# Hybrid attention and mLSTM encoder on one core: PSUM banks of the neighbourhood attention dealt out anew

## The chip, the cores and the metric

The kernel runs on one core of a Trainium2 chip. The metric is the device time of one execution in microseconds (us); "before" is the median of three runs. The core has a matrix engine (TensorE, PE in the profile), three engines for elementwise work (VectorE = DVE, ScalarE = ACT, GpSimd = POOL) and SyncE (SP), which issues most DMA transfers. PE writes its results to PSUM, which is used here as eight banks of 512 fp32 values for each of 128 partitions. DVE and ACT read them from there.

## What is computed

One encoder layer over two sequences, of 1024 and 2048 tokens, with 16 learned tokens put ahead of each. One projection feeds two branches, a 2-D neighbourhood attention and a bidirectional mLSTM; both are gated, projected, merged and sent through an output projection. The change is in the attention, which in the reference is:

```python
def row_block(r):
    r0 = jnp.clip(r - wr // 2, 0, rows - wr)
    k_blk = lax.dynamic_slice_in_dim(kg, r0, wr, axis=1)[:, :, kc]
    v_blk = lax.dynamic_slice_in_dim(vg, r0, wr, axis=1)[:, :, kc]
    s_win = jnp.einsum('bcqhd,bwckhd->bhcqwk', q_blk, k_blk).astype(jnp.float32) * scale
    s_win = jnp.where(valid[:, :, None, :], s_win + bias, NEG)
    s_met = jnp.einsum('bcqhd,bmhd->bhcqm', q_blk, km).astype(jnp.float32) * scale
    p = jax.nn.softmax(jnp.concatenate([s_met, s_win], axis=-1), axis=-1).astype(v.dtype)
    ...
    return (jnp.einsum('bhcqm,bmhd->bcqhd', p_met, vm)
            + jnp.einsum('bhcqwk,bwckhd->bcqhd', p_win, v_blk))
```

The tokens form a grid 64 wide. Each has 8 heads of 64 and looks at a window of 8 rows by 16 columns and at the 16 learned tokens.

## The kernel before

Two generators make the program. One is "dense": the projections, the gates, the merge and the output (`PLAN`), all with accumulations in three banks, pj. The other is "sparse": the mLSTM and the attention of the short sequence, then those of the long one (`STEPS`). `run` takes a piece of the sparse work, which gives its cost in us, and then dense pieces worth that much, so that attention and dense matmuls lie between each other on PE. PE executes them in just the order of the code. The orders of ACT, DVE, POOL and SP come from a scheduler, which works with estimated times when the program is built (`tc.manual_schedule(engines={PE})`, `schedule_with_timeline_sim=True`). So these orders can differ from the code's. The eight PSUM banks are named by tag:

```python
BANKS = dict(pj=3, tr=2, sc=1, sm=2)
```

`psum(tag, shape)` takes a bank of a tag; where a tag has two banks, the scheduler gives the one that comes free first by its estimate, and makes the first write wait for the last reader of what lay there.

The attention (`na`, with `STEPS`: two row tiles of the short sequence, four of the long one) works in units. A row tile is 8 grid rows; a unit is one tile, one head and one block of 16 columns: 128 queries. Each head of each tile has four units, so there are 64 units for the short sequence and 128 for the long one. A round of the loop over u has four steps, each followed by dense work of some us:

1. In odd rounds the sums of the finished pair are copied (`na_copy`, L1295, ACT). `na_scores` of unit u: it takes a bank and makes two matmuls (L1241, L1242) of split-precision queries and keys; DVE adds the bias in place and finds the extreme value (L1245). At the first unit of a head, `na_prep` starts the loads and splits of the next head (stk, kx, vr: L1189 to L1226).
2. `na_exp` of unit u on ACT reads the bank and writes prb to SBUF (L1256). This is the last read of the scores' bank. `na_scale` of unit u-1 on DVE (L1265, L1266). In odd rounds the two adds of the finished pair (`na_add`, L1302, DVE), the last reads of the sums' bank.
3. `na_turn` of unit u-2: three or four transposes on PE of prb into a bank (L1273), and an ACT copy of it to pts (L1275).
4. `na_low` of unit u-2 on DVE, the rest of the split (L1280), the last read of the transposes' bank. `na_out` of unit u-3: three or four matmuls (L1288), which sum values over the weights pts. Two units share one bank; it is taken in odd rounds.

The two calls that take banks for scores and transposes, and the one for the sums:

```python
self.turns = not self.turns
sc = self.psum("sc" if self.turns else "sm", [P, 512])      # na_scores
pt = self.psum("tr", [P, 4, P])                             # na_turn
pairs[u - 3] = self.psum("sm", [P, 512])                    # na, odd rounds
```

So even units' scores lie in sc, odd units' in one of the two sm, from which the sums also take theirs. The mLSTM (`ml`, between the attentions and ahead of the first) uses sc, tr and sm too. Its transfers are issued by `self.mq`, which is GpSimd for the long sequence and SyncE for the short one, in both kernels.

Of the kernel before, what the change touches and what calls it, by code (L numbers as in the profile page):

```python
# [3 lines left out]

# [1 line left out]

# [12 lines left out]
P = 128  # L19
# [56 lines left out]
def _row_types(R):  # L76

    out = []
    for t in range(R // 8):
        if t == 0:  # L80
            out.append((0, 0, 11))
        elif t == R // 8 - 1:
            out.append((2, R - 12, 12))
        else:
            out.append((1, 8 * t - 4, 15))
    return out
# [52 lines left out]
class K:  # L139
# [3 lines left out]
    def __init__(self, tc, ins, outs):  # L143
        self.tc, self.nc = tc, tc.nc
        self.xs = []
        self.i, self.o = ins, outs
        self.wreq, self.wraw, self.wrdy, self.wout = deque(), deque(), deque(), 0
        self.wseen, self.wkept, self.xkept = set(), {}, {}
        self.rwait = {}
        self.xput, self.turn, self.last, self.turns = deque(), 0, None, False  # L150
        self.marks, self.loose = {}, True
        self.need = False
        self.hold, self.early = deque(), True
        self.sides, self.qd, self.TD = [], {}, {}
# [949 lines left out]
    def na(self, s, rts):  # L1104

        tc, nc, i = self.tc, self.nc, self.i
        rows = _row_types(SEQLEN[s] // 64)
        with tc.tile_pool(name=f"na{s}{rts[0]}", bufs=1, side="right", reuse_waits="tile") as np_:
            self.qB = [np_.tile([P, 4, P], F32R, name=f"qB{j}") for j in range(2)]
            self.kx = [np_.tile([P, 16, 64], F32R, name=f"kx{j}") for j in range(2)]  # L1110
            self.gts = [np_.tile([P, 17, 48], F32, name=f"gt{j}") for j in range(2)]
            for q in self.qB:
                nc.gpsimd.dma_start(q[64:128], i["onehot"].rearrange("a (b c) -> a b c", b=4))
            for g in self.gts:
                nc.gpsimd.memset(g[:, 0, :], 0.0)
                nc.gpsimd.memset(g[:, 16, :], 0.0)
            heads = [(rt, pr, hh) for rt in rts for pr in range(4) for hh in range(2)]
            n = len(heads)
            prep = self.na_prep(np_, s, rows, heads, 0)
            self.na_bias(rows, heads, 0)  # L1120
            for k in range(6):
                next(prep, None)
                for _ in range(2 if k else 17 - 5 * s):
                    yield A_N[s]
            cur, nxt = self.head, None
            units = [(j, cb) for j in range(n) for cb in range(4)]
            ready = {}
            n_ = len(units)
            pairs = {}
            for u in range(n_ + 4):  # L1130
                if u >= 5 and u % 2:
                    self.na_copy(ready[u - 5], pairs[u - 5])
                    if u > n_:
                        self.na_add(ready[u - 5], pairs.pop(u - 5), s)
                if u < n_:
                    j, cb = units[u]
                    if cb == 0:
                        cur = self.head
                        prep = self.na_prep(np_, s, rows, heads, j + 1) if j + 1 < n else iter(())
                        next(prep, None)  # L1140
                    ready[u] = [cur, heads[j], cb, None, None, self.gts[j % 2], None]
                    self.na_scores(np_, ready[u], rows)
                    if j + 1 < n and cb == 0:
                        self.na_bias(rows, heads, j + 1)
                yield A_N[s]
                if u < n_:
                    self.na_exp(np_, ready[u])
                if 1 <= u <= n_:
                    self.na_scale(np_, ready[u - 1])
                if 5 <= u <= n_ and u % 2:  # L1150
                    self.na_add(ready[u - 5], pairs.pop(u - 5), s)
                if u < n_ and cb:
                    next(prep, None)
                if u == n_ + 3:
                    break
                yield A_N[s]
                if 2 <= u <= n_ + 1:
                    self.na_turn(np_, ready[u - 2])
                    if u < n_ and cb >= 2:
                        next(prep, None)  # L1160
                yield A_N[s]
                if 2 <= u <= n_ + 1:
                    self.na_low(ready[u - 2])
                if u >= 3:
                    if u % 2:
                        pairs[u - 3] = self.psum("sm", [P, 512])
                    self.na_out(ready[u - 3], pairs[(u - 3) // 2 * 2])
                yield A_N[s]
# [61 lines left out]
    def na_scores(self, np_, unit, rows):  # L1230
        nc = self.nc
        (stk, qb, kd, vt, yg, zt), (rt, pr, hh), cb = unit[:3]
        gt, c0 = unit[5], OFFC[cb] + 1
        typ, _, nr = rows[rt]
        ns = nr + 1
        kc, nb, g0 = KC0[cb], NKB[cb], (5, 1, 0)[typ]
        w, N = 8 * nb, 8 * nb * ns
        self.turns = not self.turns
        sc = self.psum("sc" if self.turns else "sm", [P, 512])
        so = sc[:, :N].rearrange("p (a b) -> p a b", b=w)  # L1240
        nc.tensor.matmul(so, stk[:, cb, :], kd[:, :ns, kc:kc + w], start=True, stop=False)  # L1241
        nc.tensor.matmul(so, qb[:, cb, :], self.kx[hh][:, :ns, kc:kc + w], start=False, stop=True)  # L1242
        pr_ = np_.tile([P, 512], F32, name="prb", bufs=3)
        mx = np_.tile([P, 1], F32, name="mx", bufs=4)
        nc.vector.tensor_tensor_reduce(  # L1245
            out=so, in0=so, in1=gt[:, g0:g0 + ns, c0:c0 + w],
            op0=ALU.add, op1=ALU.min, scale=-1.0, scalar=3.0e38, accum_out=mx)
        unit[3] = (pr_, mx, nb, 8 * ns)
        unit[6] = sc
# [18 lines left out]
    def na_turn(self, np_, unit):  # L1268
        nc = self.nc
        pr_, _, nb, ks = unit[3]  # L1270
        pt = self.psum("tr", [P, 4, P])
        for ch in range(nb):
            nc.tensor.transpose(pt[:ks, ch, :], pr_[:, ch * ks:(ch + 1) * ks], self.ident)  # L1273
        pts = np_.tile([P, 4, 2, P], F32R, name="pts", bufs=2)
        nc.scalar.activation(pts[:ks, :nb, 0, :], pt[:ks, :nb], AF.Copy)  # L1275
        unit[4], unit[6] = pts, pt
# [931 lines left out]
```

## Time and profile before

| | |
|---|---|
| median of three runs | 2667.29 us (2664.7 to 2668.91) |
| the profiled execution's own time | 2669.63 us |
| its span, first to last instruction | 2667.9 us |
| PE / DVE / ACT / POOL busy | 2633.8 / 1912.9 / 1422.4 / 365.8 us |
| mean granted clock of PE | 0.998 |
| DMA | 800.48 MB, mean 300 GB/s |
| attention of the short sequence: first to last scores | 822.0 to 1160.5 us |
| attention of the long sequence: first to last scores | 1918.4 to 2543.4 us |

The profile is of one execution. Times of rows are us from the span's start; where a row of a group gives a mean, it is in ns. In a row of the timeline stand start, length, engine, line, operation, what is written and read, and how many instructions are merged; in brackets, the idle time before it and what ended that. Matmuls overlap and their ends are modelled, so an idle time of PE is somewhat smaller than the time lost. A row of the windows view gives, for a stretch, its length and the busy time of PE, PE's weight loads, DVE, ACT and POOL with their instructions in parentheses, then PE's granted clock, the busy share of the DMA engines and GB/s.

### The profile page before, as it was taken

The numbers are of one execution on the slowest core, as the hardware profiler recorded it, in microseconds if no ns is written. First come the engines' busy times: TensorE is split into PE (matmuls) and PEld (weight loads), VectorE is DVE, ScalarE is ACT, GpSimd is POOL, SyncE is SP. The second block draws the span as 40 slices with busy tenths as digits, with TensorE's granted clock in tenths as the row PEclk, the third lists the DMA queues.
The fourth block names the chain that finished last, engine by engine and source line by source line (L and its number), as shares of the span: only waits on it lengthen the run. The fifth ranks groups of instructions, "written<-read, shape, count | busy, mean of one in ns | idle before, by whom it ended". The sixth has DMA issues, their size and how long they took to land.

```text
span 2667.9 us, 46714 instructions
## 1 busy us (share of the span) xinstructions
PE 2633.8 (99%) x15928; PEld 2326.9 (87%) x15928; DVE 1912.9 (72%) x5082; ACT 1422.4 (53%) x3292; POOL 365.8 (14%) x670
## 2 busy tenths in 40 slices
PE   9999999999999999999999999999999999999998
PEld 7998897889988999888888888888889898989888
DVE  5655678778776877546676776767478979797854
ACT  5423555544445555546665666656456555656521
POOL 0111130001301124002222222222000000000000
PEclk9999999999999999999999999999999999999999
DMA  9899988799866999978889998899899898998965
GB/s 374 329 332 338 331 298 305 276 327 351 313 215 240 353 323 307 319 226 278 260 276 363 347 287 257 283 351 355 281 308 326 276 288 277 282 310 268 333 238 203
DMA packets 346990, 800.48 MB, mean 300 GB/s; under 512 B 50016, under 2 KB 119664, under 8 KB 342912
## 3 DMA queue, kind: packets, MB, share of 16 engines
q1 hardware_dynamic: 301632, 659.35, 73.2%
q0 software_dynamic: 45120, 138.15, 15.2%
q8 instruction: 126, 2.06, 0.3%
q14 instruction: 112, 0.92, 0.1%
HBM read 543.72 MB, written 253.60 MB: 299 GB/s over the span
## 4 chain that ended last, share of the span: by engine, by line
PE 91%; DMA 4%; DVE 3%; ACT 2%; issue 1%; SPq 0%; DVEq 0%; ACTq 0%
PE pj L218 11%; PE pj L220 10%; PE pj L219 10%; PE pj L988 7%; PE pj L990 7%; PE pj L989 7%; PE pj L787 5%; PE pj L789 5%; PE pj L788 5%; PE pj L1955 3%; PE sm L1288 3%; PE pj L1954 3%; PE pj L1956 3%; PE tr L1273 2%; DMA whl<-w 1%; DMA stk<-nq 1%
## 5 line engine op out<-in xcount | busy, mean ns | idle before, releaser
L218 PE MATMUL pj<-xh,whl 128*128 128x512 f32 (+1 forms) x960 | 368.6, 384 | 2.7 <-DMA whl<-w 1.4
L220 PE MATMUL pj<-xh,whl 128*128 128x512 f32 (+1 forms) x960 | 360.4, 375 | 0.0
L219 PE MATMUL pj<-xl,whl 128*128 128x512 f32 (+1 forms) x960 | 359.8, 375 | 0.2 <-DVE xl L446 0.2
L787 PE MATMUL pj<-whl,xh 128*128 128x256 f32 (+1 forms) x1152 | 329.1, 286 | 1.7 <-DMA whl<-w 1.7
L789 PE MATMUL pj<-whl,xl 128*128 128x256 f32 (+1 forms) x1152 | 325.3, 282 | 0.0
L788 PE MATMUL pj<-whl,xh 128*128 128x256 f32 (+1 forms) x1152 | 324.9, 282 | 0.0
L1954 PE MATMUL pj<-whl,mh 128*128 128x256 f32 x768 | 218.9, 285 | 1.1 <-DMA whl<-w 1.1
L787 PEld LDWEIGHTS pj<-whl,xh 128*128 128x128 f32 x1152 | 217.1, 188 | 2.3 <-DMA whl<-w 1.9
L788 PEld LDWEIGHTS pj<-whl,xh 128*128 128x128 f32 x1152 | 217.0, 188 | 0.2
L789 PEld LDWEIGHTS pj<-whl,xl 128*128 128x128 f32 x1152 | 217.0, 188 | 0.0
L1955 PE MATMUL pj<-whl,mh 128*128 128x256 f32 x768 | 216.9, 282 | 0.0
L1956 PE MATMUL pj<-whl,mlo 128*128 128x256 f32 x768 | 216.0, 281 | 0.0
L220 PEld LDWEIGHTS pj<-xh,whl 128*128 128x128 f32 x960 | 180.9, 188 | 34.9
L218 PEld LDWEIGHTS pj<-xh,whl 128*128 128x128 f32 x960 | 180.8, 188 | 34.3 <-ACT xh L445 2.2
L988 PE MATMUL pj<-xh,whl 128*128 128x512 f32 x512 | 207.0, 404 | 1.6 <-ACT pj L1005 1.3
L219 PEld LDWEIGHTS pj<-xl,whl 128*128 128x128 f32 x960 | 181.3, 189 | 30.4 <-issue 1.0
L990 PE MATMUL pj<-xh,whl 128*128 128x512 f32 x512 | 202.0, 394 | 0.0
L989 PE MATMUL pj<-xl,whl 128*128 128x512 f32 x512 | 201.1, 393 | 0.0
L1275 ACT ACTIVATE pts<-tr 96x384 fp32r<-96x384 f32 (+2 forms) x192 | 103.4, 538 | 117.4 <-PE tr L1273 116.7
L1280 DVE TENSOR_TENSOR pts<-tr,pts 96x384 fp32r<-96x384 f32 (+2 forms) x192 | 118.6, 618 | 59.9 <-ACT pts L1275 58.3
L218 PE MATMUL pj<-yh,whl 128*128 128x512 f32 x384 | 154.1, 401 | 0.0
L219 PE MATMUL pj<-yl,whl 128*128 128x512 f32 x384 | 151.5, 394 | 0.7 <-DVE yl L1856 0.7
(387 smaller groups left out, 6993.1 us busy)
## 6 DMA issues: line engine op xcount, KB each, us to landing
whl<-w SPq DMA_DIRECT2D x131, 1024.0 KB
whl<-q SPq DMA_DIRECT2D x112, 512.0 KB
w<-whl SPq DMA_DIRECT2D x36, 1024.0 KB
wraw<-wu SPq DMA_DIRECT2D x48, 512.0 KB
gt<-st SPq DMA_DIRECT2D x96, 256.0 KB
tg<-gt SPq DMA_DIRECT2D x96, 256.0 KB
q<-po POOLq DMA_DIRECT2D x26, 512.0 KB, 7.1
xt<-xt SPq DMA_DIRECT2D x24, 512.0 KB
```

The source lines that it names most:

```text
L218: mm(out, ah, bh, start=start, stop=False)
L219: mm(out, ah, bl, start=False, stop=False)
L220: mm(out, al, bh, start=False, stop=stop)
L787: nc.tensor.matmul(o, xh, wh, start=k == 0, stop=False)
L788: nc.tensor.matmul(o, xh, wl, start=False, stop=False)
L789: nc.tensor.matmul(o, xl, wh, start=False, stop=k == KT - 1)
L988: mm(bank, w[:, 0, k], xh[:, k], start=fresh and k == 0, stop=False, skip_group_check=True)
L989: mm(bank, w[:, 0, k], xl[:, k], start=False, stop=False, skip_group_check=True)
L990: mm(bank, w[:, 1, k], xh[:, k], start=False, stop=k == 3, skip_group_check=True)
L1954: nc.tensor.matmul(o, mh[:, k, xs], wh, start=clear > 0 and k == 0, stop=False)
L1955: nc.tensor.matmul(o, mh[:, k, xs], wl, start=False, stop=False)
L1956: nc.tensor.matmul(o, ml[:, k, xs], wh, start=False, stop=clear < 2 and k == KT - 1)
```

## The change

Scores and transposes take one bank each in turn from sc, tr, tr; the turn begins anew with each call of `na`. Only the sums of pairs still take sm in the attention. The transposes' tile is now a 512 wide bank seen as 4 x 128. The number of banks for each tag, the mLSTM and the dense work stay as they are, and so does the long mLSTM's `self.mq`.

```diff
-from itertools import chain
+from itertools import chain, cycle
...
-        self.xput, self.turn, self.last, self.turns = deque(), 0, None, False
+        self.xput, self.turn, self.last = deque(), 0, None
...
                 nc.gpsimd.memset(g[:, 16, :], 0.0)
+            self.banks = cycle(("sc", "tr", "tr"))
             heads = [(rt, pr, hh) for rt in rts for pr in range(4) for hh in range(2)]
...
         w, N = 8 * nb, 8 * nb * ns
-        self.turns = not self.turns
-        sc = self.psum("sc" if self.turns else "sm", [P, 512])
+        sc = self.psum(next(self.banks), [P, 512])
         so = sc[:, :N].rearrange("p (a b) -> p a b", b=w)
...
         pr_, _, nb, ks = unit[3]
-        pt = self.psum("tr", [P, 4, P])
+        pt = self.psum(next(self.banks), [P, 512]).rearrange("p (a b) -> p a b", a=4)
         for ch in range(nb):
             nc.tensor.transpose(pt[:ks, ch, :], pr_[:, ch * ks:(ch + 1) * ks], self.ident)
```

In the prediction S(u) stands for the scores of unit u, T(u) for its transposes; "sums" are the matmuls of L1288.

## The prediction

> **What bounds the kernel now.** I read the page's head first, then the stages, then what TensorE (PE) waited for.
>
> ```profile
> PE 2633.8 (99%) x15928; PEld 2326.9 (87%) x15928; DVE 1912.9 (72%) x5082; ACT 1422.4 (53%) x3292; POOL 365.8 (14%) x670
> ```
>
> Of the 2667.9 us span PE is busy for all but 34 us. No other engine can gain the kernel more than PE's waits and its slow-clock time hold. The two attention stages:
>
> ```profile
> 820.00:1135.00 315.00, 314.72 (x2152) 291.45 (x2151) 230.05 (x522) 172.13 (x340) 63.78 (x112) 1.00 0.91 314
> ...
> 1905.00:2565.00 660.00, 651.78 (x4229) 589.33 (x4228) 533.86 (x1258) 382.06 (x871) 2.06 (x4) 1.00 0.93 291
> ```
>
> In the short one (820 to 1135) PE idles 0.3 us, in the long one (1905 to 2565) 8.2 us. The view of PE's waits (us in total, times, longest) says on whom, for 1900 to 2560:
>
> ```profile
> PE sm L1288 <- ACT prb L1256: 3.8, 6, 1.2
> PE sm L1288 <- DVE yg L1302: 3.6, 3, 2.5
> PE sm L1288 <- DVE pts L1280: 0.9, 1, 0.9
> ```
>
> They are all of the stage's waits, ten, and all are of L1288, the attention's sums. Six end with an exponential on ScalarE (ACT; prb, L1256), three with an add of finished sums on VectorE (DVE; yg, L1302), one with the sums' own data (pts, L1280). Only the last is a need for data. The other nine wait for a bank: L1256 is the last reader of a score bank, L1302 of a sum bank, so the sums do take banks which scores have just left.
>
> ```profile
> L1241 PE MATMUL sc<-kd,stk 128*128 128x288 f32 (+2 forms) x96 | 32.8, 342 | 0.0
> ...
> L1241 PE MATMUL sm<-kd,stk 128*128 128x384 f32 (+2 forms) x96 | 32.6, 340 | 0.0
> ```
>
> Of 192 units' scores, 96 lie on sc and 96 on sm, where the sums also go. The transposes, on tr, stand in no row of the waits.
>
> **What one such wait costs.** The longest, and the clock around it:
>
> ```profile
> 2170.24 0.60 PE L1273 MATMUL tr<-ident,prb 128*128 128x128 f32 x4
> 2173.32 0.59 PE L1288 MATMUL sm<-pts,vt 128*128 128x256 f32 x3 [2.48 <-DVE yg L1302]
> ...
> 2177.51 0.28 PE L1955 MATMUL pj<-whl,mh 128*128 128x256 f32 x1
> 2177.63 0.28 PE L1956 MATMUL pj<-whl,mlo 128*128 128x256 f32 x1
> ...
> 2178.45 0.60 PE L1273 MATMUL tr<-ident,prb 128*128 128x128 f32 x4
> 2178.80 0.36 PE L1954 MATMUL pj<-whl,mh 128*128 128x256 f32 x1
> ```
>
> ```profile
> 2172.75 0.42 DVE L1302 TENSOR_TENSOR yg<-sm,yg 64x256 f32<-64x256 f32 x1
> ```
>
> ```profile
> 2170.00:2175.00 5.00, 2.52 (x18) 2.32 (x17) 4.46 (x10) 3.30 (x7) 0.00 (x0) 0.89 1.02 369
> 2175.00:2180.00 5.00, 5.00 (x35) 5.00 (x35) 2.54 (x8) 2.02 (x7) 0.00 (x0) 0.77 1.02 232
> ```
>
> The add ends at 2172.75 + 0.42 = 2173.17, the sum starts at 2173.32. After four transposes the next matmul normally starts 0.35 later (2178.45 to 2178.80), so here at 2170.59: the loss is 2.73, 0.25 more than the 2.48 shown, since matmul ends are modelled. After a projection matmul (0.28 long, next one 0.12 later) a wait hides 0.16. So the nine hide 1.4 to 2.3; three follow transposes and six a projection matmul, which gives 1.7. Then the clock sinks: the granted share, 0.89 and 0.77 in two stretches of 5 us, gives 5 x 0.11 + 5 x 0.23 = 1.7 us of lost clock. So this wait cost 4.4 us in all.
>
> [...]
>
> **The change part by part.**
>
> 1. PE's stream is the code's own order and no matmul, copy or DMA is added, removed or moved, on SP's and POOL's queues neither; the loads of the long mLSTM are not in the diff. What can change are waits, and through them the order that the scheduler gives ACT and DVE.
>
> 2. Sums get both sm banks alone. A pair of units holds one for two units' time, so the next pair takes the other, last read two pairs before. How long before that one was read out, at the tightest of the long stage's 62 pairs:
>
> ```profile
> 2110.87 0.41 DVE L1302 TENSOR_TENSOR yg<-sm,yg 64x256 f32<-64x256 f32 x1
> ...
> 2119.56 0.72 PE L1288 MATMUL sm<-pts,vt 128*128 128x256 f32 x4
> ```
>
> 2119.56 - 2111.28 = 8.3 us. All nine waits go: 3.8 + 3.6 = 7.4 shown and 1.7 hidden are 9.1 us. With the 2.48 goes its slow spell, 1.7. Gross: **10.8 us**. What is late next at these places is the sums' data, as at 2166.61 below.
>
> 3. Scores and transposes share three banks in the order S(u), T(u-2), S(u+1), T(u-1), S(u+2). Every bank is taken again at the third take. S(u+2) gets the bank of T(u-2), whose last reader is the subtraction L1280; the sum of unit u-2 stands ahead of S(u+2) on PE and needs that subtraction anyway, so this wait is free. T(u-1) gets the bank of S(u) and waits for its exponential: this is new. Behind a waiting transpose PE holds the projections, everything else in its queue. Before, the bank of an even unit's scores was next needed by S(u+2), two steps later; an odd unit's by the sums of its own round, three steps earlier. So odd units gain time, even units lose some. How much is left, with the rows as they stand:
>
> ```profile
> 2146.70 0.67 ACT L1256 ACTIVATE prb<-sc,mx 128x512 f32<-128x512 f32 x1
> 2148.68 0.60 PE L1273 MATMUL tr<-ident,prb 128*128 128x128 f32 x4
> ...
> 2177.73 0.58 ACT L1256 ACTIVATE prb<-sc,mx 128x384 f32<-128x384 f32 x1 [3.81 <-DVE mx L1245]
> 2184.07 0.49 PE L1273 MATMUL tr<-ident,prb 128*128 128x128 f32 x3
> ```
>
> Over the long stage's 126 units, from the end of exponential u to the start of T(u-1), the tightest is the first pair, 2148.68 - 2147.37 = 1.3 us, the widest the second, 2184.07 - 2178.31 = 5.8; ten lie under 3. None is negative, so as they stand the new waits cost 0. Bounds: 0 below (a wait cannot gain), above the 16 us of the slow rival. The row to go by is the kernel's one wait for pts, 0.9 + 0.16: I take one such wait more, **1.1 us**, for the new order on ACT and DVE.
>
> 4. Something is bound to the DMAs rather than to PE:
>
> ```profile
> 2110.00:2160.00 50.00, 49.15 (x291) 42.56 (x290) 45.10 (x100) 24.35 (x52) 0.00 (x0) 1.00 1.02 319
> ...
> 2163.57 0.63 ACT L1208 ACTIVATE qB<-stk 64x512 fp32r<-64x512 f32 x1 [4.88 <-DMA stk<-nq]
> ...
> 2166.61 0.62 PE L1288 MATMUL sm<-pts,vt 128*128 128x256 f32 x3 [0.92 <-DVE pts L1280]
> ```
>
> ACT stood 4.88 us for stk, in the stretch where the DMA engines were full (share 1.02). PE's 2166.61 wait follows from it. A gain made inside that stretch meets the same landing and comes back as a longer wait there. From 2110 to 2160 PE's waits are this one:
>
> ```profile
> PE sm L1288 <- ACT prb L1256: 0.8, 1, 0.8
> ```
>
> With its hidden 0.16, **1.0 us** is given back. The earlier gains lie before 2110; I take it that their shift reaches the DMAs too.
>
> 5. The long mLSTM between the attention stages keeps its banks' names, but its ACT and DVE order may shift. Its neighbour of the same kind bounds it:
>
> ```profile
> PE sm L220 <- DVE ktl L1579: 4.9, 3, 2.6
> ```
>
> ```profile
> PE sm L220 <- DVE ktl L1579: 0.7, 2, 0.4
> ```
>
> 0.7 us now, 4.9 in the short mLSTM: from -0.7 to +4.2. I take 0, its own row.
>
> Sum: 10.8 - 1.1 - 1.0 = 8.7 us less. From the profiled execution's own 2669.63: 2660.9. That execution lies 2.3 above the median of the three runs, 2667.29, and its slow spell (1.7) may be part of the difference. From the median, 8.7 less gives 2658.6; if the median's run never had the spell, 2660.3 and, at the most, 2660.9. I forecast **2659.8**, 0.28% under the median.
>
> **The rivals.**
>
> *Given back (faster by less than 0.2%, 2663.4).* The waits are symptoms of late ACT and DVE, and PE meets them again at pts. For it:
>
> ```profile
> 2210.00:2260.00 50.00, 48.80 (x256) 40.81 (x256) 47.36 (x112) 27.30 (x58) 0.00 (x0) 1.00 0.87 284
> ```
>
> ```profile
> PE sm L1288 <- ACT prb L1256: 1.2, 2, 0.7
> ```
>
> DVE was busy 47.4 of 50 us here (waits in the second row), 45.1 in the stretch of 2110 to 2160. If it is the bound there, the waits in both stretches stay (0.8 + 1.2 + 3 x 0.16 = 2.5), and the 4.4 of 2173.32, whose root is the stk landing, returns as wait for pts: 6.9 of the 10.8 stay, 3.9 are gained, 2663.4. Against it: over the stage DVE is busy 533.9 of 660, and at 2173.32 pts had long been made.
>
> *The transposes pay (slower).* If the exponentials end later against PE by a fixed lag, the shortfalls of the 126 units add to 7.3 us for a lag of 3.0, 15.2 for 3.6 and 20.5 for 3.8. It decides from 3.6 on: 16 us eat the 10.8 and 0.2%. At 3.8: 2667.3 - 10.8 + 20.5 = 2677.0. For it: without the bank waits PE no longer pauses for ACT. Against: a lag of 3.6 is as much as the widest 5.8 down to 2.2, in all units at once, and ACT is idle 278 of 660 us.
>
> *The clock trips more often (2674).* If transposes stop PE for short whiles in each turn of the three banks, PE may sit at half clock again and again. A wait of 2.5 with its spell costs 4.4; four in place of the nine give 17.6 - 10.8 = 6.8 more. Against: waits up to 1.2 were followed by no slow spell here, and five banks left the clock at 1.00 over the long stage, rounded, with its one spell in it. [...]
>
> *No effect (2667).* If the sums find a free bank anyway, as in the short stage with its 0 such waits, and late engines are only dealt out anew, nothing is seen.
>
> **How the numbers follow.** Forecast 0.60, given back 0.26, no effect 0.06, transposes 0.05, clock 0.03. A measurement of this kernel (runs 2664.7 to 2668.91) can tell about 0.2%, 5.3 us, from no change. The forecast's own range goes from 2654.5 (all 10.8, and 2 us of other waits such as the mLSTM's 0.7 and the remaining pts 1.1) to 2661.9. To leave out no more than 2 in 10 it reaches over "given back" and up to no effect: 2654.5 to 2667.5. Faster: the 0.60 and a little of the second, 0.62; same 0.30; slower 0.08.
>
> **What would show it.** Right: no wait of sums for prb or yg; scores and transposes on sc and tr, the sums alone on sm; the granted clock 1.00 from 2165 on; PE's idle time in the long stage from 8.2 to about 3. Step 3 is wrong if L1273 shows waits for L1256 of more than 1 us together, step 4 if the pts wait after the stk landing is not longer. The prediction fails if waits for pts or for prb at the transposes add up to more than 5 us, or if the long mLSTM's waits grow to the short one's.

## The result and the profile after

| | before | after |
|---|---|---|
| median (lowest to highest), us | 2667.9 (2661.06 to 2669.53), 6 runs | 2657.11 (2655.07 to 2659.13), 6 runs |
| profiled execution: own time / span, us | 2669.63 / 2667.9 | 2657.13 / 2655.4 |
| long attention, first to last scores, us | 625.0 | 612.5 |

The ratio is 0.9964, with an interval of 0.9951 to 0.9977: 0.36% faster. The two profiled executions differ by 12.5 us, and the long attention alone by 12.5. What lies around it stays within 1.4 us (an mLSTM counted from its first transposes, L1575, to the first scores of the attention behind it): 521.9 and 520.6 us for the short mLSTM, 338.5 and 339.4 for the short attention, 693.2 and 693.8 for the long mLSTM. The head of the page after:

```profile
PE 2628.3 (99%) x15928; PEld 2325.4 (88%) x15928; DVE 1911.7 (72%) x5082; ACT 1421.8 (54%) x3292; POOL 365.5 (14%) x670
```

PE is busy 5.5 us less. The other 7.0 of the 12.5 us were idle time. The windows of the two attention stages (columns as before):

```profile
820.00:1135.00 315.00, 314.11 (x2148) 290.77 (x2147) 229.84 (x522) 171.84 (x340) 63.50 (x112) 1.00 0.92 312
...
1905.00:2555.00 650.00, 649.65 (x4251) 590.80 (x4250) 534.24 (x1261) 383.37 (x875) 2.07 (x4) 1.00 0.93 296
```

In the long one PE now idles 0.35 us, where it was 8.2. The first and the last scores that mark the stage, in the timeline of after:

```profile
1918.59 0.30 PE L1241 MATMUL sc<-kd,stk 128*128 128x288 f32 x1
...
2531.08 0.31 PE L1241 MATMUL sc<-kd,stk 128*128 128x312 f32 x1
```

The view of PE's waits of after, over the whole span, has one row that belongs to the attention:

```profile
PE sm L1288 <- DVE pts L1280: 0.3, 1, 0.3
```

No row has prb or yg as its releaser, and no transpose and no score waits. The groups of instructions show the new banks: scores 128 times on tr and 64 on sc, transposes 446 and 226, and none of them with idle time ahead. The sums are alone on sm:

```profile
L1288 PE MATMUL sm<-pts,vt 96*128 96x256 f32 (+2 forms) x672 | 115.3, 288 | 0.3 <-DVE pts L1280 0.3
L1273 PE MATMUL tr<-ident,prb 128*96 128x128 f32 (+2 forms) x446 | 69.3, 272 | 0.0
L1241 PE MATMUL tr<-kd,stk 128*128 128x384 f32 (+4 forms) x128 | 43.6, 341 | 0.0
L1273 PE MATMUL sc<-ident,prb 128*96 128x128 f32 (+2 forms) x226 | 35.2, 272 | 0.0
L1241 PE MATMUL sc<-kd,stk 128*128 128x384 f32 (+4 forms) x64 | 21.6, 338 | 0.0
```

The granted clock is 1.00 also where it had sunk to 0.89 and 0.77. Windows of after:

```profile
2165.00:2170.00 5.00, 5.00 (x44) 5.00 (x44) 4.57 (x10) 3.16 (x6) 0.00 (x0) 1.00 0.99 386
2170.00:2175.00 5.00, 5.00 (x43) 4.91 (x43) 4.19 (x12) 3.00 (x11) 0.00 (x0) 1.00 1.05 202
2175.00:2180.00 5.00, 5.00 (x43) 4.90 (x42) 4.62 (x11) 4.24 (x11) 0.00 (x0) 1.00 1.08 305
```

### The profile page after: what moved, and what is told of

It is laid out like the page before. It is cut to its first block, busy times and chain, and to the rows that moved or that the text cites. A ratio compares the mean times of both kernels' runs of the same rounds, so it can differ in the third digit from the quotient of the medians.

```text
span 2655.4 us, 46687 instructions
## 1 busy us (share of the span) xinstructions
PE 2628.3 (99%) x15928; PEld 2325.4 (88%) x15928; DVE 1911.7 (72%) x5082; ACT 1421.8 (54%) x3292; POOL 365.5 (14%) x670
## 5 line engine op out<-in xcount | busy, mean ns | idle before, releaser
L218 PE MATMUL pj<-yh,whl 128*128 128x512 f32 x384 | 154.1, 401 | 0.0
L220 PE MATMUL pj<-yh,whl 128*128 128x512 f32 x384 | 152.1, 396 | 0.0
L1954 PEld LDWEIGHTS pj<-whl,mh 128*128 128x128 f32 x768 | 144.7, 188 | 2.0 <-DMA whl<-w 1.2
```

The source lines that it names most:

```text
L218: mm(out, ah, bh, start=start, stop=False)
L220: mm(out, al, bh, start=False, stop=stop)
L1954: nc.tensor.matmul(o, mh[:, k, xs], wh, start=clear > 0 and k == 0, stop=False)
```

## The experiments

Theory 1: nearly the whole gain is the sums' waits for banks that scores or earlier sums still hold, with what hangs on these waits. Theory 2: the edit makes the scheduler draw new orders for ACT and DVE, and it is this luck that moved the time. An account goes with theory 1: the long attention takes 612 us plus PE's shown waits, plus about 0.2 us that each hides, plus 1.7 us for each spell of half clock in it. The 612 is the changed kernel's own 612.5 without its one wait, so only the other kernels test the account. For before it gives 612 + 8.3 + 1.9 + 1.7 = 623.9, and 625.0 was measured. The missing 1.1 is about what holds too short to be shown as waits make up: by the starts of the matmuls, the second matmul of a sum came late by about 0.09 us 55 times before (4.9 us) and 42 times after (3.6 us). What causes these holds is not shown.

### The odd-even choice turned round (before, other units on sm)

```diff
-        sc = self.psum("sc" if self.turns else "sm", [P, 512])
+        sc = self.psum("sm" if self.turns else "sc", [P, 512])
```

> The kernel before with one word exchanged: even units' scores take sm, odd units' take sc. Scores and sums still share sm, transposes keep tr, nothing is taken three in turn. The sums of an odd round then follow a score of the round before, whose exponential ended a round ago, and the next even unit's scores take the bank that the adds have left, three steps later; in the trace of before that leaves 2.2 us at the median and -0.7 at the tightest. Theory 1 (the gain is the sums' waits for banks and the slow clock behind the longest of them, nothing else): waits of sums for prb and yg gone, one to six short waits of scores for yg of 0.1 to 0.7 us, 7 to 10 us under before. Rival (the gain needs sums alone on two banks, or scores and transposes on three): within 3 us of before.

Median 2666.84 us (2663.07 to 2672.31), ratio 1.0013 (1.0004 to 1.0022): no gain at all, where 7 to 10 us were expected. The sums' waits are gone as expected. The waits of the long attention and, below them, of the short one, are now the scores':

```profile
PE sm L1241 <- DVE yg L1302: 2.6, 2, 1.4
PE sm L1241 <- DVE sm L1265: 1.8, 1, 1.8
```

```profile
PE sm L1241 <- DVE yg L1302: 2.1, 3, 0.9
```

Scores that find both sm banks with sums in them wait for the adds. The second row is such a wait too: the trace names the instruction that ended last ahead of it, a reciprocal (L1265, on a tile in SBUF that is also called sm), but an add had ended at 2230.37, 0.07 us earlier. The account gives 612 + 4.4 + 0.6 + 1.7 (a spell at 2231.8) = 618.7 us for the long attention, and 619.2 was measured. The short one took 2.8 more than before. Which units share with the sums only decides who waits.

### All scores on one bank (before, the sums alone on sm)

```diff
-        sc = self.psum("sc" if self.turns else "sm", [P, 512])
+        sc = self.psum("sc", [P, 512])
```

> The kernel before with all scores on sc; transposes keep tr, so only the sums' part of the change is made: they have sm alone. Theory 1: no wait of sums for a bank; each unit's scores now wait for the exponential of the unit before, 2.1 us of room at the median, short by 3.4 us in all over 6 units in the trace of the changed kernel: 6 to 9 us under before, and scores waiting for prb in about six places. Rival (three banks in turn are what counts): over 5 us slower than that, at the time of before or above it.

Median 2662.06 (2660.26 to 2668.14), ratio 0.9997 (0.9987 to 1.0006). Waits of PE in the long attention, and the last row in the short one:

```profile
PE sc L1241 <- ACT prb L1256: 2.6, 5, 1.3
PE sm L1288 <- DVE pts L1280: 0.6, 1, 0.6
PE pj L988 <- ACT pj L1015: 0.5, 1, 0.5
```

```profile
PE sc L1241 <- ACT prb L1256: 1.1, 1, 1.1
```

The sums wait for no bank, but scores wait for the exponential of the unit ahead, and the long attention takes 617.1 us, between before (625.0, and 620.4 to 621.6 below) and after (612.5). The account gives 612 + 3.7 + 1.4 = 617.1. In the median this gain is not seen, and the 6 to 9 us that were expected were missed: in this profile the short attention took 339.9 us (338.5 before) and the long mLSTM 695.3 (693.2), and before itself was faster beside these runs, with a median of 2662.91. What separates it from the changed kernel, 4.6 us, is about what these waits of the scores make up, so the rest of the gain needs the transposes' banks shared with the scores.

### One bank for all sums (after, sm not in turn)

```diff
             self.banks = cycle(("sc", "tr", "tr"))
+            bank = self.psum("sm", [P, 512])
...
-                        pairs[u - 3] = self.psum("sm", [P, 512])
+                        pairs[u - 3] = bank
```

> The changed kernel with one PSUM bank for the sums of all pairs; scores and transposes keep their three in turn, the second sm lies idle in the attention. Each pair's sums wait for the adds of the pair before. In the trace of the changed kernel 20 pairs would fall short, 23 us together, four of them by over 2 us, each of which would bring a slow spell of 1.7. Theory 1: waits of sums for yg come back, 10 to 25 us over the changed kernel, so at the time of before or up to 15 above. Rival (three banks for scores and transposes make the gain): stays within 3 us of the changed kernel, 2657.

Median 2679.63 (2675.65 to 2682.34), ratio 1.0055 (1.0043 to 1.0067), 22 us over the changed kernel. Its waits in the long attention (L1289 are the sums, L1303 the adds):

```profile
PE sm L1289 <- DVE yg L1303: 8.1, 8, 1.9
PE sm L1289 <- DVE sm L1266: 2.4, 3, 1.3
PE sm L1289 <- ACT sqj L1961: 1.0, 1, 1.0
```

All twelve are waits for the adds, whatever instruction the row names: an add (L1303) ended 0.14 or 0.15 us ahead of each of these sums. With the turn of three kept and the turn of two undone, PE waits 11.5 us for the sums' bank, and one spell follows (2136.7 to 2140.1). The account, with 0.2 for each of 12 waits, gives 612 + 11.5 + 2.4 + 1.7 = 627.6; 628.0 was measured. So both halves of the change are needed.

### The turn begun elsewhere (after)

```diff
-            self.banks = cycle(("sc", "tr", "tr"))
+            self.banks = cycle(("tr", "tr", "sc"))
```

> The changed kernel with the turn begun one place on (tr, tr, sc): the same banks, the same room between readers and writers, only other names, so that the scheduler makes its orders for ACT and DVE anew. Theory 1: 2657 within 2.5 us. Rival (the gain is one lucky new order): anywhere between 2657 and 2668, with other waits in the long attention than the changed kernel's single one of 0.3.

Median 2657.04 (2654.57 to 2658.76), ratio 0.9974 (0.9963 to 0.9985). Two of three takes have another tag than in the changed kernel, and the long attention takes 612.57 against 612.49 us. Its one wait:

```profile
PE sm L1288 <- DVE pts L1280: 0.4, 1, 0.4
```

This shows that the names of the banks don't matter and that the time comes back, but it doesn't test theory 2: by the traces ACT, DVE and POOL work through the same lines in the same order as in the changed kernel, from the first instruction to the last, so nothing was drawn anew. Against theory 2 speak the three runs above. Their orders of ACT and DVE in the long attention are neither those of before nor those of after, and their times follow their waits (618.7, 617.1 and 627.6 us by the account, 619.2, 617.1 and 628.0 measured).

The traces of before and after settle it. With the order of before, the banks of the change would have been free each time: the prediction's own rows leave 8.3 us for the sums and 1.3 for the transposes, and the scores have 1.9 us at the tightest. With the order of after, the banks of before would not. At unit 48 the sum, the second add of the pair before and the exponential of the round's scores stand so in after:

```profile
2165.42 0.60 PE L1288 MATMUL sm<-pts,vt 128*128 128x256 f32 x3
```

```profile
2167.58 0.42 DVE L1302 TENSOR_TENSOR yg<-sm,yg 64x256 f32<-64x256 f32 x1
```

```profile
2167.58 0.58 ACT L1256 ACTIVATE prb<-tr,mx 128x384 f32<-128x384 f32 x1 [0.53 <-DVE mx L1245]
```

In before one sm bank would hold that pair and the other those scores, so the sum could not have started until 2168.00, 2.6 us later. Even if each sum takes the bank that comes free first, seven sums of the long attention in after start ahead of that, by 5.6 us together. So ACT and DVE are still late there; the change takes away that PE has to wait for them. Theory 2 falls by this.

The four kernels so far ran beside 24 runs of before with a median of 2662.91, lower than in the first comparison, which leads to the next question.

### The kernel before, twice more

> The kernel before, unchanged, for a second profile. In the first its long attention took 625.0 us from first to last scores against 612.5 in the changed kernel, while its runs beside the last experiments had a median of 2662.9. Theory 1a (the waits of the sums for banks hang on when loads land, and the slow clock on how a wait lies, so both differ from one execution to the next): the long attention takes 615 to 622 us here where the time is near 2663, with waits for prb and yg between 3 and 7 us and perhaps no slow spell; all other stages within 1.5 us of the first profile. Rival (another chip is a little faster as a whole): every stage shorter by the same 0.2%.

> The kernel before once more, a third profile, with the same expectations: theory 1a puts nearly all of the difference between executions of it into the long attention's waits for prb and yg and into slow spells of 1.7 us; the rival spreads it over all stages.

2664.16 and 2662.53 us, with long attentions of 621.6 and 620.4 us against 625.0. So the long attention has 3.5 of the 5.5 us and 4.7 of the 7.1 us by which these spans are shorter than the first; the short mLSTM has 1.5 and 2.7, the other stages 0.4 or less. That is nearer to the expectation than to its rival, a chip that is faster in all stages alike. The waits there, of the one and then of the other:

```profile
PE sm L1288 <- ACT prb L1256: 4.0, 6, 1.2
PE sm L1288 <- DVE yg L1302: 2.9, 2, 1.8
```

```profile
PE sm L1288 <- ACT prb L1256: 3.4, 5, 1.2
PE sm L1288 <- DVE yg L1302: 2.1, 2, 1.5
```

The waits for prb come back at the same five units with the same lengths (unit 20: 1.16 us in all three executions; a sixth comes and goes). Those for yg do not. At unit 48 it is 2.48, 1.79 and 1.54 us, in step with the wait of ACT for stk ahead of it: 4.88, 3.01 and 2.76. Of these only the longest had the clock sink behind it (to 0.89 and 0.77 in two windows), though length alone doesn't decide: with the odd-even choice turned round and with one bank for all sums, waits of 1.8 and 1.9 us had a spell. What tells them apart is not shown. The landing of stk differs from one execution to the next, and in before it reaches PE through this wait. After has a stk wait of 4.32 at this place and no bank wait behind it.

### The finish of the transposes repeated, 6 and 13 times (after)

At six units of the long attention `na_low`, which writes the same result again, is done five and twelve times more, to make sums wait for their data for a known time.

```diff
                     self.na_low(ready[u - 2])
+                    if s and u - 2 in (16, 32, 48, 64, 80, 96):
+                        for _ in range(5):
+                            self.na_low(ready[u - 2])
```

> The changed kernel with VectorE's subtraction for the transposes (L1280) done six times and not once at six units of the long attention, 16 units apart; the outcome is the same each time. Five more of 0.61 us delay those units' sums by 3.1 us, where the room was 3.7 at the median. Theory 1: waits of 0 to 1 us at these places and no slow spell: 0 to 4 us over the changed kernel. Rival (VectorE is the bound of the stage): its 18 us more go into the time, 10 us or more.

> The same with thirteen subtractions at the six units: 7.3 us more each, beyond the room of 3.7. Theory 1 with the price of a long wait as forecast (the wait itself, and 1.7 us of half clock behind most of them): six waits of sums for pts of 3 to 4 us, four to six slow spells, 25 to 35 us over the changed kernel. Rival (no slow spell behind a wait of this size, the clock's fall at 2173.9 had another cause): 18 to 24 us over, and a clock at 1.00. VectorE as the bound: 44 us.

2710.87 us (2706.18 to 2714.1), ratio 1.0166 (1.0148 to 1.0184), and 2734.78 (2733.64 to 2737.82), ratio 1.0261 (1.0244 to 1.0278): 54 and 78 us over the changed kernel, far over what was expected. PE's waits in the long attention with five more (L1291 are the sums, L1283 is `na_low`), then with twelve:

```profile
PE sm L1291 <- DVE pts L1283: 22.5, 5, 7.7
PE sm L1291 <- DVE nwy L162: 5.9, 1, 5.9
PE sm L1291 <- ACT sqj L1963: 4.9, 1, 4.9
```

```profile
PE sm L1291 <- DVE pts L1283: 39.6, 4, 11.8
PE sm L1291 <- DVE nwy L167: 20.0, 2, 10.1
```

That is 33.3 us in seven waits, one of them of 0.2 us and the others at the six units, and 59.6 us in six. Whatever instruction a row names, a subtraction (L1283) ended 0.05 to 0.15 us ahead of each of these sums. The first place with five more, in the timeline of DVE:

```profile
2005.94 1.14 DVE L1283 TENSOR_TENSOR pts<-tr,pts 96x384 fp32r<-96x384 f32 x2
...
2008.42 0.55 DVE L1283 TENSOR_TENSOR pts<-tr,pts 96x384 fp32r<-96x384 f32 x1
...
2011.04 1.14 DVE L1283 TENSOR_TENSOR pts<-tr,pts 96x384 fp32r<-96x384 f32 x2
2012.11 0.15 DVE L1268 RECIPROCAL sm<-sm 128x1 f32<-128x1 f32 x1
2012.18 0.67 DVE L1307 TENSOR_TENSOR yg<-yg,zt 128x512 f32<-128x512 f32 x1
2012.77 0.68 DVE L1924 TENSOR_TENSOR tg<-tg 128x512 f32<-128x512 f32 x1
2013.37 0.55 DVE L1283 TENSOR_TENSOR pts<-tr,pts 96x384 fp32r<-96x384 f32 x1
...
2014.11 0.55 DVE L1283 TENSOR_TENSOR pts<-tr,pts 96x384 fp32r<-96x384 f32 x1
```

```profile
2014.81 0.98 PE L1291 MATMUL sm<-pts,vt 96*128 96x256 f32 x3 [4.17 <-DVE pts L1283]
```

The six subtractions of unit 16, some 0.55 us each, are not done in a row (the second of the two at 2011.04 is that of unit 17). From 2005.94 to 2014.66 the six take 3.3 of 8.7 us, the rest is other work that the scheduler put between them, and the sum that needed them came at 2014.81. Then the clock (windows of the same kernel):

```profile
2010.00:2015.00 5.00, 0.82 (x4) 0.41 (x3) 4.97 (x11) 0.97 (x3) 0.00 (x0) 0.90 0.99 247
2015.00:2020.00 5.00, 5.00 (x15) 4.13 (x16) 1.38 (x4) 0.47 (x2) 0.00 (x0) 0.50 0.98 275
2020.00:2025.00 5.00, 5.00 (x26) 4.22 (x25) 3.02 (x8) 1.55 (x5) 0.00 (x0) 0.92 0.46 136
```

The granted share is 0.90, 0.50 and 0.92: 0.5 + 2.5 + 0.4 = 3.4 us of clock, the first 0.4 of it while PE stood still. Each of the six long waits had such a spell, 6.8 us long five times and 10.2 once. What they took after the waits' ends adds up to 14.7 us. 33.3 + 1.3 hidden + 14.7 = 49.3, and the long attention grew by 47.7. With twelve more there are spells of 10.2 to 13.7 us, and the mean granted clock of the execution is 0.985 (0.99 with five more). The expectation's mechanism, a wait and then a spell, is there. Its size failed on the length of the wait, which depends on what else DVE has in its order. The rival, VectorE as the bound of the stage, named 10 us or more and 44 and so came nearer; but the added work of DVE is 18 and 44 us, and the long attention grew by 47.7 and 74.0.

### The changed kernel again, and a subtraction moved to GpSimd

> The changed kernel, unchanged, beside the kernel before on one chip. Theory 1 from the three profiles of before (long attention 625.0, 621.6, 620.4 us against 612.5): 7 to 12 us under before at the median, and a smaller spread than before's, since the waits that hung on landings are gone. Rival (the first comparison's 10.8 was the chip's doing): under 5 us.

2654.76 us (2653.11 to 2663.68), ratio 0.9961 (0.9947 to 0.9976), and a long attention of 612.54 us: the result comes back. The smaller spread that was expected does not: with one run of 2663.68 us it is as wide as that of before (2662.08 to 2672.75).

```diff
-                nc.vector.tensor_tensor(x[1][:, 2 * e:2 * e + 2, :512], xts[e], h.bitcast(F32), op=ALU.subtract)
+                nc.gpsimd.tensor_tensor(x[1][:, 2 * e:2 * e + 2, :512], xts[e], h.bitcast(F32), op=ALU.subtract)
```

This was an attempt at a faster version, since the largest wait left stands in the short mLSTM, where DVE is late with ktl.

> The changed kernel with the four subtractions of each projection input's split (L542; 128x1024, 1.2 us each on VectorE) on GpSimd, which is idle about them; PE's order is the same. The longest wait that is left in the changed kernel is one of 2.6 us at 440 for a subtraction of the short mLSTM (ktl), which stands on VectorE behind three of these, and a slow spell often follows it. If the price list holds (wait, 0.2 hidden, 1.7 for a spell), taking it away gains 2.8 to 4.5 us: 2653 to 2655. Against it: if GpSimd takes over 3 us for each, the next projection waits for its input (xl) and the gain is lost.

2671.2 us (2667.95 to 2676.47), 16 us slower than the changed kernel beside it, where 2653 to 2655 was expected. GpSimd took 2.4 us for a subtraction, less than the 3 us that the expectation feared; the time went another way. DVE's, POOL's and PE's rows of the kernel with the move, then DVE's row of the changed kernel for the same three instructions:

```profile
434.91 10.14 DVE L1552 SCALAR_TENSOR_TENSOR vwl<-va,g_wT,vwh 128x130 fp32r<-128x130 f32 x3
```

```profile
434.72 2.41 POOL L542 TENSOR_TENSOR xl<-xt,xh 128x1024 fp32r<-128x1024 f32 x1 [14.01 <-ACT xh L541]
...
437.68 6.94 POOL L542 TENSOR_TENSOR xl<-xt,xh 128x1024 fp32r<-128x1024 f32 x3
```

```profile
446.71 0.58 PE L220 MATMUL sm<-vwh,ktl 128*128 128x260 f32 x1 [8.48 <-DVE ktl L1579]
```

```profile
434.00 0.88 DVE L1552 SCALAR_TENSOR_TENSOR vwl<-va,g_wT,vwh 128x130 fp32r<-128x130 f32 x3
```

While POOL subtracts from 434.72 to 444.6, three DVE instructions take 10.14 us by the trace that take 0.88 without it, and PE waits 8.48 us for ktl behind them. A spell of 10.2 us goes with this wait, another of 6.8 us with a wait of 2.31 us at 777, and the short mLSTM takes 536.8 us instead of 520. What holds the three up is not shown beyond this coincidence in time. The long attention stays at 612.1, the same as without the move. No version tried here is faster than the changed kernel.

## Why the prediction was right, and where its steps were not

The forecast, 2659.8, lies 2.7 above the median; the gain of the medians is 10.8 us where 7.5 was forecast. The mechanism is the one forecast, but the steps were 4.0 us too small together, and that the number came so near is in part luck: the profiled execution from which the steps were priced took longer than any of the six runs of before, 2669.63 against 2669.53 us and less. Beside other runs of before it was 11.5 for the changed kernel again, and 5.9 for the one with the turn begun elsewhere.

*Step 1 held.* The stages outside the attention moved by 1.4 us at most.

*Step 2 held, with its size.* The nine bank waits went, and the spell. That the spell was there to be gained was luck: the two later profiles of before have none in the long attention. Beside the waits the step did not count the short holds inside sums, 1.3 us. The run with one bank for all sums shows that the second one is needed, and that with all scores on one bank that keeping the scores off sm is not enough by itself.

*Step 3 was too careful.* The 1.1 us for a new wait was not spent. No transpose waits for an exponential, though the room is smaller: 1.3 us at the tightest before, and 0.85 after (unit 51). That the new order brings one more wait for data was not borne out; one such wait stands, 0.35 us, and it is the old one.

*Step 4 was wrong.* It took it that what is gained between 2110 and 2160 leaves the landing of stk where it is and returns there as a longer wait. ACT's and PE's rows of after at this place, and the issue of that transfer by SP in the two kernels, after first:

```profile
2158.39 0.63 ACT L1209 ACTIVATE qB<-stk 64x512 fp32r<-64x512 f32 x1 [4.32 <-DMA stk<-nq]
...
2161.43 0.63 PE L1288 MATMUL sm<-pts,vt 128*128 128x256 f32 x3 [0.35 <-DVE pts L1280]
```

```profile
2145.78 0.48 SPq L1190 DMA_DIRECT2D stk<-nq  x1
```

```profile
2150.80 0.59 SPq L1189 DMA_DIRECT2D stk<-nq  x1
```

The transfer is issued 5.0 us earlier, as all else runs earlier, and lands earlier: ACT starts on it 12.6 us after the issue in after (2158.39 - 2145.78) and 12.8 in before (2163.57 - 2150.80). ACT's wait goes from 4.88 to 4.32 and PE's from 0.92 to 0.35. Instead of 1.0 given back, 0.6 is gained. The prediction's own sign for a failure, a pts wait not longer, is what came.

*Step 5 held:* the long mLSTM went from 693.2 to 693.8 us.

With these, the sum closes for the profiled executions: 8.7 + 1.1 + 1.0 + 0.6 + 1.3 = 12.7, against 12.5 measured. That the median gained less than this, 10.8, is because the profiled execution of before lay 1.7 above its median and had the longest yg wait and a spell in it; the two later ones of before had 3.5 to 4.7 us less in the long attention.

*The rivals.* "Given back" fails on the absent wait at unit 48: by the rows of 2165.42 above, its sums found bank and data while ACT and DVE were as late as before. "The clock trips more often" needed short stops of PE at the transposes, and there are none. "The transposes pay" fails by the same rows; in the changed kernel 13 of the 127 units have less than 3 us of room, against ten before, and none is negative. "No effect" fits the short attention only (338.5 us before, 339.4 after, with 0.6 of it a wait for weights). The prediction left open, with its 2660.3 (7.0 under the median: the 8.7 without the spell's 1.7), whether a spell can be absent in another execution of the same kernel. The short mLSTM shows it: in the three profiles of before PE waits 2.64 us for ktl, up to 439.96, 440.24 and 440.44; a spell follows from about 440 on in the first two, where projection matmuls behind the wait start 0.43 us apart, and none in the third, where they start 0.23 apart. Row of the third:

```profile
440.44 0.39 PE L220 MATMUL sm<-vwh,ktl 128*128 128x260 f32 x1 [2.64 <-DVE ktl L1579]
```

The long wait at unit 48 is no such case, since it was itself shorter where no spell followed.

What stays open: a bank wait of 2.5 us with its spell was seen in one of three profiles of before, and how often it comes in the executions that were not profiled isn't known. The median of before was 2667.9, 2662.91, 2666.38 and 2666.21 us in the four comparisons, and why it was lower in the second is not shown. In the long attention the gain is 12.5 us against the first profile and 9.1 and 7.9 against the two others.

## What to carry to other kernels

Where an in-order engine fills banks for several readers, look in the trace at each bank's last read and next write: the group that keeps a bank longest should have banks of its own, and the short-lived groups can share the rest in turn, if the needed release comes from something the engine waits for anyway, or lies well ahead of it (0.85 us at the tightest here). Moving the sharing to other members of the long-lived group's banks moves only the wait, as with the odd-even choice turned round. Before costing a wait behind a transfer as fixed, see whether the issue of the transfer shifts with the gain.

## What was unexpected of the hardware

Leaving out the first 15 and the last 22 us of each execution, the spells of half clock lasted 3.4 us with waits of 1.8 to 2.64 us, 6.8 with waits of 3.7 to 6.8 (once with 2.3), 10.2 with waits of 7.7 to 10.1, and 13.7 with waits of 9.9 to 11.8. In the first profile of before the granted clock is 0.50 from 439.90 and again from 2173.87, for 3.41 us each, and in the profile of after from 440.78, for 3.41. With five more subtractions the spells added 14.7 us to 33.3 of waiting.

The wait of 2.64 us for ktl had a spell behind it in two of the three profiles of before, and the waits at unit 48 had one behind 2.48 us and none behind 1.79 and 1.54. What decides is not shown.

The same code differed by up to 4.7 us in one stage of before, in good part through a bank wait that hangs on the landing of a transfer and the spell behind it; the two profiles of the changed kernel differ there by 0.05. And the same three DVE instructions took 10.14 us beside GpSimd's subtractions and 0.88 without them.
